# A hybrid encoder on one Trainium2 core: probabilities transposed one chunk of keys at a time for both heads, and wider dead products at the start

## The chip, the cores and the metric

One core of one Trainium2 chip runs the whole program. TensorE multiplies and transposes, and writes PSUM; VectorE, ScalarE and GpSimd do elementwise work; SyncE starts the transfers. The metric is the device time of one execution in microseconds. An engine takes its instructions in the order in which they were written; between engines, semaphores hold an instruction back until its operands are there.

## What is computed

Two layers of an encoder over a prompt of 512 tokens and a sample of 256, with 1024 features, fp32. In each layer 16 query heads of 64, two to a key head, are split among three mixers: global attention, neighbourhood attention with a learned bias, and attention over three dilated windows. Then come an output projection and a gated feed-forward part.

```python
def encoder_trunk(x, ...):
    for l in range(DEPTH):
        h = rms_norm(x, norm_mix[l])
        proj = h @ w_in[l]
        q, k, v = ...                          # 16 query heads, 8 key and value heads
        o_a = dense_block_attention(q_a, k_a, v_a)              # all keys
        o_b, _ = gathered_block_attention(q_b, k_b, v_b, na_idx, bias_b)
        branches = [gathered_block_attention(q_c, k_c, v_c, idx, bias) for (idx, bias) in dil]
        o_c = ...                              # merged by the softmax denominators
        y = jnp.concatenate([rms_norm(o, out_gain) for o in (o_a, o_b, o_c)], axis=-1)
        x = x + y @ w_out[l]
        h = rms_norm(x, norm_ffn[l])
        gate, up = jnp.split(h @ w_gate_up[l], 2, axis=-1)
        x = x + (jax.nn.silu(gate) * up) @ w_down[l]

def block(qi):                                 # 128 queries
    s = jnp.einsum('bqhgd,bkhd->bhgqk', qi, k) * scale
    p = jax.nn.softmax(s, axis=-1)
    return jnp.einsum('bhgqk,bkhd->bqhgd', p, v)
```

## The kernel before

The 768 tokens lie in three passes p of 256: p = 0 and 1 are the prompt, p = 2 is the sample. A *group* g is one key head with its two query heads h; a layer has eight, and the program takes the three neighbourhood groups first (mixer m = 1), then the three dilated ones (m = 2), then the two global ones (m = 0). Every fp32 number that enters a product is split into a high part, rounded to the type fp32r, and the rest, so a projection is three products (`mm3`, L617 to L619).

For each group `emit_qkv` makes queries, keys and values: 48 products of 256 columns for each pass, norms and rotation on VectorE, ScalarE and GpSimd, then transposes of the queries (L885) and keys (L889). `emit_attn` (L905 on) does the attention of a group, pass by pass. For a head h and a block j of 128 queries it forms the scores over 256 or 512 keys (L953, two products), finds the maximum on VectorE (L959; L997 for the masked mixers, which writes the masked scores into a tile P) and takes the exponential on ScalarE (L961 or L1000) into P. When both blocks of a head have their P, two chunks of 128 keys of both blocks are transposed into one bank of PSUM (L1012, four transposes, pool PT), ScalarE copies the bank rounded (L1019), VectorE subtracts that from the bank (L1020; both in a buffer of pool PTS), and four products of 256 columns (L1034) multiply the values with these probabilities:

```python
                        for z, c in enumerate(cs):
                            ...
                            v = vals(gs, pp)[:, jj]
                            for i in range(2):
                                end = z == len(cs) - 1 and i == 1
                                PE.matmul(po[0][:, o:o + wd], v, ps_[i][:, z * wd:(z + 1) * wd],
```

The values carry their high part and their rest side by side, so the result has 128 rows, which ScalarE (L1044) and VectorE (L1049) add up; a spread of the softmax sums (L1061) scales it. In the neighbourhood groups the two blocks of a prompt pass see different keys: two chunks are common, and each block has a third of its own, a group of one chunk and one block with products of 128 columns. The output projection of a mixer follows its last group (L617 to L619 from `yt`), with sums of squares by products with ones (L626 exact, L637 split). Then come the feed-forward products of 384 columns.

Pools matter for the order: two banks for scores (S), two for transposes (PT), one for the attention's result (PO), two for projections (D), one for small things (M); four P tiles, three PTS buffers. The order is no one's by hand: every operation is given to a planner (`Plan`) with a priority and an assumed cost, which places operations on the engines at build time, allots buffers, and writes each engine's list once. So any change of an operation moves others. The last group of a layer has no next projection beside it.

At the start, TensorE multiplies a tile of ones by itself 26 times (`warmup`, L543, `WARM`), 128 columns each, before any operand has arrived; nothing reads the result. VectorE sets the ones (L536).

Of the kernel before, what the change touches and what calls it, by code (L numbers as in the profile page):

```python
# [27 lines left out]
FIRST_F = 2  # L28
EPS = 1e-6
NEG = -1e30  # L30
WARM = 26
NSTK = 1
RW = 127
GROUPS = ((0, 1), (2, 3, 4), (5, 6, 7))
# [337 lines left out]
def trunk(ctx: ExitStack, tc: tile.TileContext, t):  # L372
# [127 lines left out]
    def ew(n, fn, r=(), w=(), prio=0.0, on="DVE POOL", act=None, fast=False, ptr=False, sbuf=True, extra=0):  # L500
        cost = {"DVE": v_cost(n, fast, ptr), "POOL": g_cost(n), "ACT": a_cost(n, sbuf, extra)}
        eng = {"DVE": DVE, "POOL": POOL}
        if on in K:
            turn[on] = turn.get(on, -1) + 1
            lst = K[on].split(",")
            on = lst[turn[on] % len(lst)]
        opts = [(e, cost[e], lambda e=e: fn(eng[e])) for e in on.split() if e != "ACT"]
        if "ACT" in on:
            opts.insert(0 if on.startswith("ACT") else len(opts), ("ACT", cost["ACT"], act))
        return P.op(opts, 0.0, None, r, w, prio, lat=0.05, lock=sbuf)  # L510

    def pe(cost, fn, r=(), w=(), prio=0.0):
        return P.op("PE", cost, fn, r, w, prio, lat=0.1)
# [22 lines left out]
    P.op("DVE", 0.2, lambda: DVE.memset(ones.bitcast(F32), 1.0), w=["ones"], prio=-100)  # L536
    act(128, lambda: ACT.copy(identr, tmp[0]), r=[tmp], w=["identr", "ident"], prio=-15)

    warm = P.buf("M")

    def warmup():
        for _ in range(WARM):
            PE.matmul(warm[0][:, 0:128], ones, ones, start=True, stop=True)  # L543

    P.op("PE", 4.0, warmup, r=["ones"], w=[warm], prio=-100)

    def load_gains(l, m, prio):
        b = P.buf("QKG")
# [254 lines left out]
    def vals(gs, p):  # L803
        return (gs[p][4 + p] if p < 2 else gs[p][3]).rearrange("p (j d) -> p j d", j=2)
# [100 lines left out]
    def emit_attn(l, g, gs, bs, mc):  # L905
# [15 lines left out]
        for p in order(g):  # L921
# [14 lines left out]
            po = P.buf("PO")  # L936
            rsum = P.buf("SM")
            rv = lambda rsum=rsum: rsum[0][:, 0:4].rearrange("p (j h) -> p j h", j=2)
            for h in range(2):
                PP = []  # L940
                for j in range(2):
                    b = 2 * p + j
                    k0, nk = 0, ncols
                    if m == 1 and p < 2:
                        k0, nk = (0, 64, 192, 256)[b], 256
                    S, pr_, mx = P.buf("S"), P.buf("P"), P.buf("SM")
                    PP.append(pr_)

                    def qk(p=p, h=h, j=j, k0=k0, nk=nk, S=S):
                        q = query(gs, p).rearrange("p (h t) -> p h t", h=2)[:, h, j * 128:(j + 1) * 128]  # L950
# [19 lines left out]
                    else:  # L970
# [29 lines left out]
                    act(nk, lambda dst=dst, mx=mx, rsl=rsl: ACT.activation(  # L1000
                        dst(), dst(), AF.Exp, bias=mx[0][:, 0:1], scale=-1.0, accum_out=rsl()),
                        r=[mx, "table"], w=[pr_, (rsum, j, h)], prio=pr, extra=2)
                grps = [((c, c + 1), (0, 1)) for c in range(0, nch - 1, 2)]
                if m == 1 and p < 2:
                    grps = [((p, p + 1), (0, 1)), ((2 - 2 * p,), (1 - p,))]
                for gi, (cs, js) in enumerate(grps):
                    n = 128 * len(cs) * len(js)
                    pt, ps_ = P.buf("PT"), P.buf("PTS")

                    def tr(cs=cs, js=js, pt=pt, PP=PP):  # L1010
                        for i, (c, j) in enumerate([(c, j) for c in cs for j in js]):
                            PE.transpose(pt[0][:, i * 128:(i + 1) * 128], PP[j][0][:, c * 128:(c + 1) * 128], ident)  # L1012

                    rr_ = [PP[j] for j in js] + [(PP[j], 1) for j in js if m == 1 and p < 2 and p != j]
                    pe(n / 128 * TR, tr, r=rr_ + ["ident"], w=[pt], prio=pr)
                    vt = [(gs[pp], "v", pp, i) for pp in ((0, 1) if p < 2 else (2,)) for i in range(2)]
                    ew(n, lambda E, n=n, pt=pt, ps_=ps_: E.tensor_copy(ps_[0][:, :n], pt[0][:, :n]), r=[pt],
                       w=[(ps_, 0)], prio=pr, sbuf=False, on="pth",
                       act=lambda n=n, pt=pt, ps_=ps_: ACT.copy(ps_[0][:, :n], pt[0][:, :n]))  # L1019
                    dve(n, lambda n=n, pt=pt, ps_=ps_: DVE.tensor_tensor(  # L1020
                        ps_[1][:, :n], pt[0][:, :n], ps_[0][:, :n].bitcast(F32), op=OP.subtract),
                        r=[pt, (ps_, 0)], w=[(ps_, 1)], prio=pr)

                    def pv(cs=cs, js=js, ps_=ps_, h=h, p=p, po=po, c0=c0, first=gi == 0, last=len(js) < 2 or gi == len(grps) - 1,
                           more=gi < len(grps) - 1 and len(grps[gi + 1][1]) < 2):
                        wd = 128 * len(js)
                        o = h * 256 + js[0] * 128
                        for z, c in enumerate(cs):
                            kb = c0 + c
                            pp, jj = (kb // 2, kb % 2) if p < 2 else (2, c)  # L1030
                            v = vals(gs, pp)[:, jj]
                            for i in range(2):
                                end = z == len(cs) - 1 and i == 1
                                PE.matmul(po[0][:, o:o + wd], v, ps_[i][:, z * wd:(z + 1) * wd],  # L1034
                                          start=first and z == 0 and i == 0, stop=end and (last or more),
                                          **({} if wd > 128 else {"skip_group_check": True}))

                    pe(2 * len(cs) * (len(js) * 128 / 2400.0 + 0.0135), pv, r=[(ps_, 0), (ps_, 1)] + vt, w=[po], prio=pr)
            yr = P.buf("Y")
            ys[m, p].append(yr)  # L1040
            for h in range(2):
# [391 lines left out]
```

## Time and profile before

| | |
|---|---|
| three runs | 1723.49, 1723.81 (median) and 1727.6 us |
| the profiled execution | 1724.8 us |
| its span, first to last instruction | 1722.9 us |
| TensorE busy | 1687.9 us (98%), 11434 products |
| VectorE, ScalarE, GpSimd busy | 1390.4, 943.7, 614.1 us |
| transfers | 145.31 MB, 84 GB/s on average |

The page gives busy times by engine, the timeline gives starts, and a wait is put down to the operation whose semaphore came last. Attention takes from about 43 to 345 us in layer 0 and from about 895 to 1203 us in layer 1; the rest is the start and the two feed-forward parts. A product's listed time overlaps with the next one's, so the distance between two starts is what one adds to TensorE's stream. Where two engines' waits meet, the one named need not be the only cause.

### The profile page before, as it was taken

What the parts mean: (1) busy time and instruction counts of PE and PEld (TensorE: products, weight loads), DVE (VectorE), ACT (ScalarE), POOL (GpSimd) and SP (SyncE); (2) the same over time, 40 slices, a digit from 0 to 9 for tenths busy, and PEclk for the clock granted to TensorE, in tenths of its full rate; (3) what the DMA queues carried; (4) which work ended last, traced back from release to release, by engine and by line L of the source; (5) the groups of instructions that cost most, each with busy time, mean ns of one, the idle gap of its engine ahead of it and who ended that gap; (6) DMA issues with size and microseconds to landing.
All of it is one profiled execution on the core that took longest, in us unless ns stands there. A gap on an engine that the chain in (4) does not pass through costs nothing. (4 is left out here: it accounts for less than half of the span.)

```text
span 1722.9 us, 31174 instructions
## 1 busy us (share of the span) xinstructions
PE 1687.9 (98%) x11434; PEld 1660.9 (96%) x11434; DVE 1390.4 (81%) x2609; ACT 943.7 (55%) x2194; POOL 614.1 (36%) x620
## 2 busy tenths in 40 slices
PE   9999999899999999999999999998999999999999
PEld 8999999899999999999999999997999999999999
DVE  7778678699988887778868886877999887868693
ACT  7877577574444444424458865866744444434230
POOL 1655254223433333224126633632242333323130
PEclk9999999999999999999999999999999999999999
DMA  6221111102433333524322201101133333334233
GB/s 182 73 69 39 38 47 40 50 31 89 132 99 103 97 103 112 155 57 130 97 64 65 77 25 38 57 26 50 47 126 101 102 101 102 108 116 138 80 111 99
DMA packets 102890, 145.31 MB, mean 84 GB/s; under 512 B 29008, under 2 KB 66896, under 8 KB 102736
## 3 DMA queue, kind: packets, MB, share of 16 engines
q1 hardware_dynamic: 102736, 143.31, 27.7%
q8 instruction: 90, 1.47, 0.4%
q14 instruction: 64, 0.52, 0.1%
HBM read 122.82 MB, written 20.45 MB: 83 GB/s over the span
## 5 line engine op out<-in xcount | busy, mean ns | idle before, releaser
L617 PE MATMUL ps<-u,w 128*128 128x384 f32 (+1 forms) x1588 | 526.8, 332 | 8.4 <-ACT y L1193 4.2
L618 PE MATMUL ps<-u,w 128*128 128x384 f32 (+1 forms) x1588 | 525.8, 331 | 0.0
L619 PE MATMUL ps<-u,w 128*128 128x384 f32 (+1 forms) x1588 | 525.6, 331 | 0.0
L617 PEld LDWEIGHTS ps<-u,w 128*128 128x128 f32 x1588 | 298.5, 188 | 11.9 <-ACT y L1193 6.4
L618 PEld LDWEIGHTS ps<-u,w 128*128 128x128 f32 x1588 | 298.5, 188 | 0.3 <-POOL u L1218 0.3
L619 PEld LDWEIGHTS ps<-u,w 128*128 128x128 f32 x1588 | 298.5, 188 | 0.0
L617 PE MATMUL ps<-w,u 128*128 128x256 f32 x768 | 227.1, 296 | 0.4 <-DVE ppa L835 0.2
L618 PE MATMUL ps<-w,u 128*128 128x256 f32 x768 | 219.4, 286 | 0.9 <-DVE w L593 0.7
L619 PE MATMUL ps<-w,u 128*128 128x256 f32 x768 | 219.2, 285 | 0.0
L618 PEld LDWEIGHTS ps<-w,u 128*128 128x128 f32 x768 | 148.6, 193 | 3.0 <-DVE w L593 2.0
L617 PEld LDWEIGHTS ps<-w,u 128*128 128x128 f32 x768 | 148.2, 193 | 2.1 <-DVE ppa L835 0.4
L592 ACT CAST w<-raw 128x1024 fp32r<-128x1024 f32 (+2 forms) x86 | 78.1, 908 | 129.6 <-PE ps L618 90.6
L619 PEld LDWEIGHTS ps<-w,u 128*128 128x128 f32 x768 | 148.4, 193 | 0.2
L1198 DVE TENSOR_TENSOR y<-y,ps 128x384 f32<-128x384 f32 x160 | 86.0, 548 | 59.9 <-PE ps L619 33.1
L617 PE MATMUL ps<-yt,w 128*128 128x256 f32 x392 | 114.1, 291 | 2.1 <-DVE x L1104 1.6
L1020 DVE TENSOR_TENSOR u<-ps,u 128x512 fp32r<-128x512 f32 (+1 forms) x160 | 98.2, 625 | 20.0 <-ACT u L1019 19.1
L618 PE MATMUL ps<-yt,w 128*128 128x256 f32 x392 | 111.8, 285 | 1.1 <-POOL yt L1090 0.8
L619 PE MATMUL ps<-yt,w 128*128 128x256 f32 x392 | 111.2, 284 | 0.0
L1034 PE MATMUL ps<-u 128*128 128x256 f32 (+1 forms) x592 | 102.9, 291 | 6.0 <-DVE u L1020 4.6
L619 PE MATMUL ps<-u,yt 128*128 128x384 f32 x292 | 97.5, 334 | 0.0
L617 PE MATMUL ps<-u,yt 128*128 128x384 f32 x292 | 97.5, 334 | 0.0
L618 PE MATMUL ps<-u,yt 128*128 128x384 f32 x292 | 97.5, 334 | 0.0
(284 smaller groups left out, 3972.3 us busy)
## 6 DMA issues: line engine op xcount, KB each, us to landing
spill<-y SPq DMA_DIRECT2D x86, 192.0 KB, 2.4
raw<-in_w_gu SPq DMA_DIRECT2D x63, 256.0 KB, 2.8
raw<-in_w_in SPq DMA_DIRECT2D x30, 512.0 KB, 3.7
p<-in_w_gu SPq DMA_DIRECT2D x44, 256.0 KB, 2.8
ppa<-in_w_gu SPq DMA_DIRECT2D x39, 256.0 KB, 2.9
raw<-in_w_out SPq DMA_DIRECT2D x16, 512.0 KB, 3.6
tbm<-in_w_gu SPq DMA_DIRECT2D x30, 256.0 KB, 2.9
raw<-in_w_down SPq DMA_DIRECT2D x16, 384.0 KB, 3.4
```

The lines of the kernel that those rows point to most:

```text
L592: act(n, lambda raw=raw, hs=hs: ACT.copy(self.flat(0)[:, hs], raw[0][:, :n]), r=[raw], w=[(b, 0) + z], prio=pr)
L617: PE.matmul(out, a[0], b[0], start=start, stop=False, skip_group_check=on)
L618: PE.matmul(out, a[0], b[1], start=False, stop=False, skip_group_check=on)
L619: PE.matmul(out, a[1], b[0], start=False, stop=stop, skip_group_check=on)
L1020: dve(n, lambda n=n, pt=pt, ps_=ps_: DVE.tensor_tensor(ps_[1][:, :n], pt[0][:, :n], ps_[0][:, :n].bitcast(F32), op=OP.subtract), r=[pt, (p ...
L1034: PE.matmul(po[0][:, o:o + wd], v, ps_[i][:, z * wd:(z + 1) * wd], start=first and z == 0 and i == 0, stop=end and (last or more), **({} i ...
L1198: dve(HALF, lambda sg=sg, dst=dst, src=src, op=op, b=bank[bn]: DVE.tensor_tensor(sg[dst], sg[src], b[0][:, :HALF], op=op), r=[bank[bn], (s ...
```

## The change

The two heads of a pass now share the transposes. Scores and exponentials are made for all four blocks (two heads, two blocks), and then one chunk of keys at a time is transposed for both heads and both blocks: four transposes into a bank as before, but with one and the same piece of the values to multiply, so two products of 512 columns take the place of four of 256. The own chunks of the neighbourhood blocks are done for both heads at once, in two products of 256 columns in place of four of 128. The lists of P tiles become `PP[h][j]`, and the loop over groups moves out of the loop over heads. The dead products take 512 columns of a tile of ones in a buffer of pool YT, set by VectorE (a new memset), and there are 15 of them.

```diff
-WARM = 26
+WARM = 15
...
-    warm = P.buf("M")
+    warm, wide = P.buf("M"), P.buf("YT")
...
         for _ in range(WARM):
-            PE.matmul(warm[0][:, 0:128], ones, ones, start=True, stop=True)
-
-    P.op("PE", 4.0, warmup, r=["ones"], w=[warm], prio=-100)
+            PE.matmul(warm[0], ones, wide[0], start=True, stop=True)
+
+    P.op("DVE", 0.35, lambda: DVE.memset(wide[0].bitcast(F32), 1.0), w=[wide], prio=-100)
+    P.op("PE", 4.0, warmup, r=["ones", wide], w=[warm], prio=-100)
...
+            PP = [[], []]
             for h in range(2):
-                PP = []
                 for j in range(2):
...
-                    PP.append(pr_)
+                    PP[h].append(pr_)
...
-                grps = [((c, c + 1), (0, 1)) for c in range(0, nch - 1, 2)]
-                if m == 1 and p < 2:
-                    grps = [((p, p + 1), (0, 1)), ((2 - 2 * p,), (1 - p,))]
-                for gi, (cs, js) in enumerate(grps):
-                    n = 128 * len(cs) * len(js)
-                    pt, ps_ = P.buf("PT"), P.buf("PTS")
-
-                    def tr(cs=cs, js=js, pt=pt, PP=PP):
-                        for i, (c, j) in enumerate([(c, j) for c in cs for j in js]):
-                            PE.transpose(pt[0][:, i * 128:(i + 1) * 128], PP[j][0][:, c * 128:(c + 1) * 128], ident)
...
+            grps = [(c, (0, 1)) for c in range(nch)]
+            if m == 1 and p < 2:
+                grps = [(p, (0, 1)), (p + 1, (0, 1)), (2 - 2 * p, (1 - p,))]
+            for gi, (c, js) in enumerate(grps):
+                full, n = len(js) == 2, 256 * len(js)
+                pt, ps_ = P.buf("PT"), P.buf("PTS")
+
+                def tr(c=c, js=js, pt=pt, PP=PP):
+                    for i, (h, j) in enumerate([(h, j) for h in range(2) for j in js]):
+                        PE.transpose(pt[0][:, i * 128:(i + 1) * 128], PP[h][j][0][:, c * 128:(c + 1) * 128], ident)
...
+                    out = po[0] if full else po[0].rearrange("p (h t) -> p h t", h=2)[:, :, js[0] * 128:js[0] * 128 + 128]
+                    for i in range(2):
+                        rhs = ps_[i][:, :n] if full else ps_[i][:, :n].rearrange("p (h t) -> p h t", h=2)
+                        PE.matmul(out, v, rhs, start=first and i == 0, stop=last and i == 1,
+                                  **({} if full else {"skip_group_check": True}))
+
+                pe(2 * (n / 2400.0 + 0.0135), pv, r=[(ps_, 0), (ps_, 1)] + vt, w=[po], prio=pr)
```

The planner's order moves with it. In these rows ps_73 and ps_74 are the banks of scores, ps_75 and ps_76 those of transposes, ps_77 the attention's result, ps_78 the small bank, ps_71 and ps_72 those of projections. In the changed kernel the scores are L954, the transposes L1013, the value products L1034, the spread L1060, and projections L618 to L620.

First place, TensorE, layer 0, last group, pass 0. Before:

```order
L953 MATMUL ps_74<-u 128x512 x2
L1061 MATMUL ps_78<-identr,sq 128x128 x2
L953 MATMUL ps_73<-u 128x512 x2
L1012 MATMUL ps_75<-identr,p 128x128 x4
L1012 MATMUL ps_76<-identr,p 128x128 x4
L953 MATMUL ps_74<-u 128x512 x2
L953 MATMUL ps_73<-u 128x512 x2
L1034 MATMUL ps_77<-u 128x256 x8
```

With the change:

```order
L1060 MATMUL ps_78<-identr,sq 128x128 x2
L954 MATMUL ps_73<-u 128x512 x2
L954 MATMUL ps_74<-u 128x512 x2
L1013 MATMUL ps_75<-identr,p 128x128 x4
L1013 MATMUL ps_76<-identr,p 128x128 x4
L954 MATMUL ps_73<-u 128x512 x2
L1034 MATMUL ps_77<-u 128x512 x2
L1013 MATMUL ps_75<-identr,p 128x128 x4
L1034 MATMUL ps_77<-u 128x512 x2
L1013 MATMUL ps_76<-identr,p 128x128 x4
L627 MATMUL ps_78<-sq,ones 128x256
L1034 MATMUL ps_77<-u 128x512 x4
```

Before, the transposes between the scores belong to the first head alone, and the last of the second head's scores stand behind them. Now all four blocks' scores of the pass stand ahead of the first transposes (the pair into ps_74 just ahead of them is already the next pass's), and value products alternate with single rows of transposes.

Second place, TensorE, layer 1, first group, between its first and second pass. Before:

```order
L1034 MATMUL ps_77<-u 128x256 x4
L1012 MATMUL ps_75<-identr,p 128x128 x4
L1034 MATMUL ps_77<-u 128x128 x2
L1012 MATMUL ps_76<-identr,p 128x128
L953 MATMUL ps_74<-u 128x256 x2
L1061 MATMUL ps_78<-identr,sq 128x128 x2
L953 MATMUL ps_73<-u 128x256 x2
L617 MATMUL ps_72<-w,u 128x256
L618 MATMUL ps_72<-w,u 128x256
L619 MATMUL ps_72<-w,u 128x256
```

With the change:

```order
L1013 MATMUL ps_76<-identr,p 128x128 x2
L1034 MATMUL ps_77<-u 128x512 x2
L954 MATMUL ps_73<-u 128x256 x2
L1034 MATMUL ps_77<-u 128x2x128 x2
L954 MATMUL ps_73<-u 128x256 x2
L1060 MATMUL ps_78<-identr,sq 128x128 x2
L954 MATMUL ps_74<-u 128x256 x2
L1013 MATMUL ps_75<-identr,p 128x128 x4
L1013 MATMUL ps_76<-identr,p 128x128 x4
L954 MATMUL ps_73<-u 128x256 x2
L1013 MATMUL ps_75<-identr,p 128x128 x2
L1034 MATMUL ps_77<-u 128x512 x4
```

Before, nine more projection products and a score pair follow the ten rows' last before the next pass's transposes. Now no projection product stands between the passes' transposes.

## Rows read from the trace of the kernel before

**Rows 1.** The page, part 1: busy time, share of the span and instructions.

```profile
PE 1687.9 (98%) x11434; PEld 1660.9 (96%) x11434; DVE 1390.4 (81%) x2609; ACT 943.7 (55%) x2194; POOL 614.1 (36%) x620
```

**Rows 2.** Stretches: length, busy time by engine (x instructions), granted clock, DMA, GB/s.

```profile
14.50:20.50 6.00, 6.00 (x30) 6.00 (x30) 6.00 (x16) 6.00 (x16) 0.00 (x0) 1.00 1.00 334
...
321.00:340.00 19.00, 15.09 (x97) 12.02 (x96) 16.64 (x28) 16.02 (x37) 6.98 (x8) 1.00 0.32 110
...
905.00:928.00 23.00, 20.97 (x176) 20.27 (x174) 19.67 (x56) 19.26 (x60) 14.43 (x23) 1.00 0.33 80
```

**Rows 3.** Groups by shape: tiles, shape, count; busy, mean ns; idle before, releasers.

```profile
L1034 PE MATMUL ps<-u 128*128 128x256 f32 x544 | 93.4, 292 | 6.0 <-DVE u L1020 4.6 <-DVE y L1049 1.2
...
L1000 ACT ACTIVATE p<-p,sm 128x256 f32<-128x256 f32 x96 | 48.6, 508 | 8.4 <-DVE sm L997 8.0
...
L1034 PE MATMUL ps<-u 128*128 128x128 f32 x48 | 9.7, 283 | 0.0
```

**Rows 4.** TensorE's timeline: start us, us, engine, line, what; layer 0, layer 1.

```profile
308.42 0.64 PE L1034 MATMUL ps<-u 128*128 128x256 f32 x4
308.90 0.28 PE L617 MATMUL ps<-yt,w 128*128 128x256 f32 x1
...
321.35 0.63 PE L953 MATMUL ps<-u 128*128 128x512 f32 x2
321.81 0.38 PE L1061 MATMUL ps<-identr,sq 128*128 128x128 f32 x2
...
336.71 0.28 PE L618 MATMUL ps<-yt,w 128*128 128x256 f32 x1
...
905.52 0.60 PE L1012 MATMUL ps<-identr,p 128*128 128x128 f32 x4
905.88 0.42 PE L1034 MATMUL ps<-u 128*128 128x128 f32 x2
906.13 0.30 PE L1012 MATMUL ps<-identr,p 128*128 128x128 f32 x1
```

**Rows 5.** TensorE's timeline, the start of the program.

```profile
1.09 5.81 PE L543 MATMUL ps<-ones 128*128 128x128 f32 x26 [1.09 <-DVE ones L536]
...
20.03 0.41 PE L618 MATMUL ps<-w,u 128*128 128x256 f32 x1
20.25 0.41 PE L619 MATMUL ps<-w,u 128*128 128x256 f32 x1
...
21.16 0.28 PE L619 MATMUL ps<-w,u 128*128 128x256 f32 x1
21.28 0.28 PE L617 MATMUL ps<-w,u 128*128 128x256 f32 x1
...
33.66 0.54 PE L885 MATMUL ps<-identr,u 128*128 128x128 f32 x4 [1.34 <-DVE u L877]
```

**Rows 6.** VectorE's timeline, the start of the program.

```profile
23.08 0.29 DVE L839 TENSOR_TENSOR vs<-ps,rbt 128x128 f32<-128x128 f32 x1 [1.99 <-ACT ppa L834]
```

**Rows 7.** Timelines of TensorE and VectorE, last group of layer 0.

```profile
326.40 0.73 PE L953 MATMUL ps<-u 128*128 128x512 f32 x2 [1.18 <-ACT p L961]
...
328.73 1.04 PE L1012 MATMUL ps<-identr,p 128*128 128x128 f32 x8
...
337.78 0.60 PE L1012 MATMUL ps<-identr,p 128*128 128x128 f32 x4
...
339.04 0.69 DVE L1020 TENSOR_TENSOR u<-ps,u 128x512 fp32r<-128x512 f32 x1 [1.28 <-ACT u L1019]
```

**Rows 8.** Waits of TensorE: total us, times, longest; 310:340, 905:928, 1174:1200.

```profile
PE ps L1012 <- ACT p L961: 1.9, 2, 1.0
PE ps L1034 <- DVE u L1020: 1.2, 2, 0.8
...
PE ps L953 <- DVE sm L997: 1.7, 1, 1.7
...
PE ps L1034 <- DVE u L1020: 1.7, 2, 1.5
```

More of the change, by code (lines that the diff above doesn't have):

```diff
@@ L1002, in emit_attn @@
                         r=[mx, "table"], w=[pr_, (rsum, j, h)], prio=pr, extra=2)
-                grps = [((c, c + 1), (0, 1)) for c in range(0, nch - 1, 2)]
-                if m == 1 and p < 2:
-                    grps = [((p, p + 1), (0, 1)), ((2 - 2 * p,), (1 - p,))]
-                for gi, (cs, js) in enumerate(grps):
-                    n = 128 * len(cs) * len(js)
-                    pt, ps_ = P.buf("PT"), P.buf("PTS")
-                    def tr(cs=cs, js=js, pt=pt, PP=PP):
-                        for i, (c, j) in enumerate([(c, j) for c in cs for j in js]):
-                            PE.transpose(pt[0][:, i * 128:(i + 1) * 128], PP[j][0][:, c * 128:(c + 1) * 128], ident)
[L1014 to L1038, printed above, removed]
@@ new lines, in emit_attn, with pv @@
+            grps = [(c, (0, 1)) for c in range(nch)]
[7 more added lines that the diff above has]
+                        PE.transpose(pt[0][:, i * 128:(i + 1) * 128], PP[h][j][0][:, c * 128:(c + 1) * 128], ident)
+                rr_ = [PP[h][j] for h in range(2) for j in js]
+                rr_ += [(PP[h][j], 1) for h in range(2) for j in js if m == 1 and p < 2 and p != j]
+                pe(n / 128 * TR, tr, r=rr_ + ["ident"], w=[pt], prio=pr)
+                vt = [(gs[pp], "v", pp, i) for pp in ((0, 1) if p < 2 else (2,)) for i in range(2)]
+                ew(n, lambda E, n=n, pt=pt, ps_=ps_: E.tensor_copy(ps_[0][:, :n], pt[0][:, :n]), r=[pt],
+                   w=[(ps_, 0)], prio=pr, sbuf=False, on="pth",
+                   act=lambda n=n, pt=pt, ps_=ps_: ACT.copy(ps_[0][:, :n], pt[0][:, :n]))
+                dve(n, lambda n=n, pt=pt, ps_=ps_: DVE.tensor_tensor(
+                    ps_[1][:, :n], pt[0][:, :n], ps_[0][:, :n].bitcast(F32), op=OP.subtract),
+                    r=[pt, (ps_, 0)], w=[(ps_, 1)], prio=pr)
+                last = gi == len(grps) - 1 or len(grps[gi + 1][1]) < 2
+                def pv(c=c, js=js, ps_=ps_, p=p, po=po, c0=c0, first=gi == 0, last=last, full=full, n=n):
+                    kb = c0 + c
+                    pp, jj = (kb // 2, kb % 2) if p < 2 else (2, c)
+                    v = vals(gs, pp)[:, jj]
+                    out = po[0] if full else po[0].rearrange("p (h t) -> p h t", h=2)[:, :, js[0] * 128:js[0] * 128 + 128]
[4 more added lines that the diff above has]
+                pe(2 * (n / 2400.0 + 0.0135), pv, r=[(ps_, 0), (ps_, 1)] + vt, w=[po], prio=pr)
```

## The prediction

> **What bounds the kernel now.** I read the page first: TensorE is busy for 98% of the span [rows 1], so what a change is worth depends on what it does to the stream of products, and on the few places where that stream waits. The page's busy time counts the pipeline of a product too (a product of 256 columns is listed with 0.28 us, yet the next one starts 0.12 us later [rows 5]), so I went on to the starts in the timeline, which show what a product costs on the path. Then I looked for waits, stage by stage. In the feed-forward stretches TensorE hardly waits. The attention stretches do wait, most of all in the last head group of a layer, where no projection of a next group is left to fill the gaps [rows 7, 8], and in the first group of layer 1 [rows 8]. There VectorE is busy for 19.67 and ScalarE for 19.26 of 23 us [rows 2], so what TensorE waits for comes through two engines that have little room. The third place is the start.
>
> **Value products.** There are 544 of 256 columns, in 136 groups of four, and 48 of 128 columns, in 24 pairs [rows 3]. Four of 256 take 0.48 us from start to the next start; the scores' two of 512 columns take 0.46 us, and they are what each group becomes [rows 4]. By these rows the change saves 0.02 us x 136 = 2.7 us. The stamps have two digits, so I also take the step apart: 0.12 us, less 256 columns at the 2.4 GHz level (0.107 us), leaves 0.013 us per product, and 272 products go: 3.6 us. I take 3.2. The Trainium skill (TensorE: Matmul & The Clock Gate, "Back-to-back issue gap") gives a fixed part of about 2.5 ns beside the columns instead; by that the term would be 272 x 0.0025 = 0.7 us and the time 2.5 us later than I forecast. The trace does not agree: its step leaves 13 ns, not 2.5.
>
> The 24 pairs of 128 columns become 12 pairs of 256, since one product now takes the odd block for both heads. A pair of 128 takes 0.25 us [rows 4], no less than a pair of 256 does (0.24), so narrow products save nothing by being narrow: 24 x 0.25 - 12 x 0.24 = 3.1 us. Some pairs stand closer in the trace; were they all at the columns alone (2 x 0.053 us), the term would be -0.3 us. I take 3.0. All of this lies on the path, because TensorE is the bound around it. Transposes keep their number. Copies and differences out of PSUM become 12 fewer pieces on ScalarE and VectorE each; I cost that at nothing, as both have other work beside it.
>
> **Dead products at the start.** Before, 26 dead products of 128 columns end near 6.9 us; real products then step by 0.21 to 0.22 us until about 20.5 us and by 0.12 us afterwards [rows 2, 5]. The granted-clock column prints 1.00 there [rows 2], so it does not tell these apart; 256 columns in 0.21 us is the 1.2 GHz level, in 0.12 us the 2.4 GHz level. The dead products too ran at the lower level (0.22 us for 128 columns), and the step fell only after some 6 us of products of 256 columns back to back. Fifteen of 512 columns at the lower level, 0.43 us each, fill 6.4 us without a break in the columns, so I expect the level to rise by their end. They start a little later (a VectorE memset of 512 columns comes ahead; VectorE is idle then, waiting for the gains' transfer) and end 1 us later at worst, which the operands' lateness until 14 us absorbs.
>
> What is that worth? From 14.5 to 20.5 us VectorE and ScalarE are busy without a gap [rows 2], and TensorE is the late one: 30 products step by 0.21 instead of 0.12 us, 2.8 us. Behind it VectorE stands idle for 1.99 us, waiting for ScalarE's square of the first group [rows 6], which cannot begin before that group's last product. After that VectorE has hardly a gap until the transposes of the first queries, which start at 33.66 us after a wait of 1.34 us for it [rows 5]. So only VectorE's 1.99 us can be gained there; the rest turns into a longer wait at those transposes. I take 2.0 us, with ends of 0 (no rise) and 3.0.
>
> **What is added: later transposes.** The first transpose of a pass now needs the exponentials of both heads, four blocks instead of two. All four P tiles come free only with the pass's last transposes, so the next pass's exponentials start later. Where other products stand between, that costs nothing; the cover is the projection of the next group, and where that is gone TensorE waits. The needs, from rows: from the end of a pair of 512-column scores to its transpose 2.33 - 0.46 = 1.87 us; from the end of four transposes to their difference on VectorE 1.95 us from the first transpose's start [rows 7], less the 0.36 us that four take [rows 4], 1.6 us. From one pass's last transposes to the next's first in the neighbourhood groups: landing and first reduction some 0.8 us, then four exponentials of 0.51 us [rows 3], about 2.9 us, an estimate.
>
> *Last group, layer 0* (first place of the order). Behind the 512-column scores stands one further pair (0.46 us) ahead of the transposes: 1.4 us short. The first value products have four transposes and a score pair ahead of them, 0.82 us: 0.8 short; the third, counted alike, 0.94 us: 0.7 short; the fourth another 0.3. The second pass lacks some 1.2. Together 4.4 us, against 3.1 us of waits of the transposes and value products shown before [rows 8]. In layer 1 the same count gives about 3 us, against 1.7 us shown there for the differences alone [rows 8]. Waits come out longer than such counts when the two engines serve other work first, so I put 1.0 us for both tails, with ends of -2 and +4.
>
> *First group of layer 1* (second place). Between the last transposes of one pass and the first of the next stand a pair of 512 (0.46 us), four pairs of 256 (0.24 each) and a spread (some 0.1), 1.5 us in all, where 2.9 are needed: 1.4 short. Then the first value products have 0.78 us of the needed 1.6: 0.8 short. One wait of 1.7 us shown there now may go. I put 1.5 us, ends 0 and 3.
>
> *Elsewhere.* Seven more passages between passes of the neighbourhood groups have a cover that exceeds the need by less than 0.6 us. ScalarE and VectorE also serve the next group's projections, so an exponential there may be late: 0.3 us each, 2.0 us, ends 0 and 6.
>
> **The sum.** -3.2 - 3.0 - 2.0 + 1.0 + 1.5 + 2.0 = -3.7 us. The profiled execution took 1724.8 us (span 1722.9), so 1721.1 us; the median of the three runs, 1723.81, is 1.0 us below that execution. A measurement tells about 0.3%, 5.2 us, from no change.
>
> **Rivals.** *Cover holds:* the scheduler puts the transposes where nothing waits, as it does in most groups before, and no net wait is added: 1724.8 - 8.2 = 1716.6. For it: only two passages lack cover by the count. Against it: tails already wait now. Chance 0.26.
>
> *The P tiles become the bound (slower):* a pass's four exponentials, four copies and four differences must then run through within one pass, since the next has no P tile to write. It decides where TensorE's work between passes is shorter than the chain in its real, queued length; with a chain 1.5 us longer than my 2.9, the seven narrow passages wait some 1.2 us each and the two that lack cover 2.9 and 1.7, 13 us, and the tails cost the 1.0 of above: 1724.8 - 8.2 + 14 = 1730.6. For it: VectorE and ScalarE are 84% busy there. Against it: most passages have over 4 us of cover. Chance 0.14.
>
> *The dead products do not do what they are for:* the level stays low until 20 us, or falls again at 8 to 14 us, where products wait for operands. Then 2.0 us are missing: 1723.1. Against a fall: in the tail of layer 0 TensorE is busy for only 15.09 of 19 us [rows 2], and a product of 256 columns is still listed with 0.28 us [rows 4], not with the 0.41 us of the lower level [rows 5]. Chance 0.15.
>
> **Chances.** My forecast has the remaining 0.45. Faster by over 0.3% means under 1718.6: the first rival and the lower part of the forecast's spread, 0.36. Slower means over 1729.0: the second rival and a little of the rest, 0.16. Within: 0.48. For the range, the low end takes the first rival with its starting term at 3.0 and 1 us of luck, 1714.5; the high end stops short of the slower rival's centre, 1729.5, which leaves out about 0.1 on each side.
>
> **What would show it.** Value products in pairs with 0.45 to 0.46 us from start to start of two; no pair of 128 columns; a step of 0.12 us by 9 us; the first query transposes near 31.5 us; waits of the transposes on exponentials (p) in the first group of layer 1, about 2 us. I am wrong if pairs of 512 take 0.48 or more, if the step is still 0.21 us at 15 us, or if waits on p turn up in all neighbourhood groups.

## The result and the profile after

The changed kernel takes 1742.41 us (median of 4 runs, 1741.67 to 1743.19); the kernel before took 1724.61 beside it. The ratio is 1.0102, 95% interval 1.009 to 1.0115: slower, and outside the predicted range. The profiled execution took 1743.19 us, span 1741.2, so 18.3 us more of span than before.

The page of the changed kernel, part 1:

```profile
PE 1695.2 (97%) x11127; PEld 1650.6 (95%) x11127; DVE 1405.9 (81%) x2612; ACT 941.8 (54%) x2184; POOL 595.1 (34%) x604
```

307 products are gone [rows 1], and yet TensorE's busy time grew by 7 us, so some products ran longer. The stretches show where (columns as in [rows 2]):

```profile
14.50:20.50 6.00, 6.00 (x32) 6.00 (x31) 6.00 (x16) 5.90 (x16) 0.00 (x0) 0.54 0.98 327
321.00:340.00 19.00, 16.02 (x97) 12.41 (x96) 17.02 (x32) 17.01 (x42) 8.99 (x10) 1.00 0.37 111
905.00:928.00 23.00, 20.48 (x146) 18.26 (x145) 17.56 (x50) 16.96 (x50) 8.90 (x17) 0.93 0.19 45
345.00:900.00 555.00, 544.33 (x3270) 541.93 (x3269) 460.14 (x741) 242.32 (x474) 160.72 (x125) 0.98 0.32 97
```

The same 555 us of the feed-forward in the kernel before:

```profile
345.00:900.00 555.00, 549.00 (x3360) 545.77 (x3359) 463.70 (x759) 251.04 (x494) 168.10 (x133) 1.00 0.33 98
```

Ninety records of TensorE fewer fit into the same stretch, which the diff doesn't touch, and the granted clock there is 0.98. What the prediction looked for is there too. The value products by shape, and one set in the timeline (two of 512 columns, 310.75 to 311.22):

```profile
L1034 PE MATMUL ps<-u 128*128 128x512 f32 x272 | 90.7, 414 | 1.8 <-DVE u L1022 1.5 <-DVE y L1048 0.2
...
L1034 PE MATMUL ps<-u 128*128 128x256 f32 x24 | 5.4, 300 | 0.8 <-DVE u L1022 0.6 <-ACT u L1021 0.2
```

```profile
310.75 0.63 PE L1034 MATMUL ps<-u 128*128 128x512 f32 x2
311.22 0.62 PE L954 MATMUL ps<-u 128*128 128x512 f32 x2
```

The start, in TensorE's timeline:

```profile
1.62 5.92 PE L543 MATMUL ps<-yt,ones 128*128 128x512 f32 x15 [1.62 <-DVE yt L545]
7.39 0.27 PE L618 MATMUL ps<-w,u 128*128 128x256 f32 x1
7.50 0.28 PE L619 MATMUL ps<-w,u 128*128 128x256 f32 x1
...
14.58 0.41 PE L619 MATMUL ps<-w,u 128*128 128x256 f32 x1
14.79 0.41 PE L620 MATMUL ps<-w,u 128*128 128x256 f32 x1
...
33.07 0.53 PE L886 MATMUL ps<-identr,u 128*128 128x128 f32 x4 [1.83 <-DVE u L878]
```

The wide dead products do raise the level: at 7.5 us a product of 256 columns steps by 0.12 us. Then operands are late, and from 14 to 20 us the step is 0.21 again, the 1.2 GHz level. The first query transposes start 0.6 us earlier than before [rows 5], not 2.

The largest single loss stands in the first feed-forward. TensorE's, VectorE's and GpSimd's timelines of the changed kernel:

```profile
800.33 0.34 PE L620 MATMUL ps<-u,yt 128*128 128x384 f32 x1
805.64 0.66 PE L618 MATMUL ps<-u,w 128*128 128x384 f32 x1 [4.98 <-DVE x L1258]
806.10 0.53 PE L619 MATMUL ps<-u,w 128*128 128x384 f32 x1
806.42 0.53 PE L620 MATMUL ps<-u,w 128*128 128x384 f32 x1
```

```profile
797.54 0.68 DVE L1134 TENSOR_TENSOR w<-p,w 128x512 fp32r<-128x512 f32 x1
...
799.07 1.69 DVE L1134 TENSOR_TENSOR w<-raw,w 128x512 fp32r<-128x512 f32 x1
800.68 1.75 DVE L1134 TENSOR_TENSOR w<-p,w 128x512 fp32r<-128x512 f32 x1
802.35 1.74 DVE L1134 TENSOR_TENSOR w<-raw,w 128x512 fp32r<-128x512 f32 x1
804.02 1.01 DVE L1236 TENSOR_TENSOR u<-tbm,u 128x384 fp32r<-128x384 f32 x2
804.96 0.54 DVE L1258 TENSOR_TENSOR x<-x,ps 128x384 f32<-128x384 f32 x1
```

```profile
798.92 1.29 POOL L1134 TENSOR_TENSOR w<-p,w 128x512 fp32r<-128x512 f32 x1 [4.13 <-ACT w L1133]
800.48 1.40 POOL L1134 TENSOR_TENSOR w<-raw,w 128x512 fp32r<-128x512 f32 x1 [0.28 <-ACT w L1133]
801.84 1.71 POOL L1134 TENSOR_TENSOR w<-ppa,w 128x512 fp32r<-128x512 f32 x1
```

TensorE has filled a bank and waits for VectorE to add it to x (L1258). From 799.07 us VectorE has three splits of weights (L1134) and two subtractions (L1236, 1.01 us together) ahead of that addition, and each split takes 1.7 us instead of 0.68: GpSimd runs the same operation beside it, and VectorE's ends 0.54 to 0.55 us after GpSimd's each time (800.76 after 800.21, 802.43 after 801.88, 804.09 after 803.55). After the wait 384 columns step by 0.32 us instead of 0.17. Another such wait of 4.06 us ends at 1672.15 us. In the kernel before, the longest waits of this kind are 1.62 and 1.59 us:

```profile
818.19 0.41 PE L617 MATMUL ps<-u,w 128*128 128x384 f32 x1 [1.62 <-DVE x L1259]
```

**Lost time by stage.** To compare orders I summed, over TensorE's timeline, each distance between two starts less the step of its kind at the upper level (0.120 us for 256 columns, 0.173 for 384, 0.227 for 512, at most 0.089 for the 128-column ones). What is left is waits, small gaps and slow steps. (0.227 is low: a value product of 512 columns behind which nothing waits steps by 0.233 us, the median of 57 pairs ahead of transposes. What that changes is said where it matters.) One profiled execution each, in us:

| kernel | 0–40 | 40–345 attention | 345–900 | 900–1260 attention | 1260– | sum |
|---|---|---|---|---|---|---|
| before | 13.6 | 23.4 | 11.6 | 27.0 | 6.8 | 82.4 |
| changed | 13.1 | 22.5 | 22.3 | 33.9 | 12.6 | 104.4 |

The products' own steps add up to 1635.2 us before and 1630.9 now; with 0.2335 us for 512 columns they are 2.4 us apart instead of 4.3. So 16.5 of the 22 us lost stand outside attention.

### The profile page after: what moved, and what is told of

Same layout as the page of the kernel before. It is cut to its first block, busy times and chain, and to the rows that moved or that the text cites. A ratio compares the mean times of both kernels' runs of the same rounds, so it can differ in the third digit from the quotient of the medians.

```text
span 1741.2 us, 30428 instructions
## 1 busy us (share of the span) xinstructions
PE 1695.2 (97%) x11127; PEld 1650.6 (95%) x11127; DVE 1405.9 (81%) x2612; ACT 941.8 (54%) x2184; POOL 595.1 (34%) x604
## 5 line engine op out<-in xcount | busy, mean ns | idle before, releaser
L618 PE MATMUL ps<-u,w 128*128 128x384 f32 (+1 forms) x1584 | 528.0, 333 | 14.0 <-DVE x L1258 10.0
L620 PE MATMUL ps<-u,w 128*128 128x384 f32 (+1 forms) x1584 | 526.1, 332 | 0.0
L618 PEld LDWEIGHTS ps<-u,w 128*128 128x128 f32 x1584 | 299.4, 189 | 17.4 <-issue 11.1
L620 PEld LDWEIGHTS ps<-u,w 128*128 128x128 f32 x1584 | 299.1, 189 | 0.0
L618 PE MATMUL ps<-w,u 128*128 128x256 f32 x768 | 229.3, 299 | 3.6 <-DVE x L1302 1.6
L620 PE MATMUL ps<-w,u 128*128 128x256 f32 x768 | 219.9, 286 | 0.0
L618 PEld LDWEIGHTS ps<-w,u 128*128 128x128 f32 x768 | 148.9, 194 | 6.5 <-DVE x L1302 1.8
L620 PEld LDWEIGHTS ps<-w,u 128*128 128x128 f32 x768 | 148.9, 194 | 0.3 <-DVE u L654 0.2
L618 PE MATMUL ps<-yt,w 128*128 128x256 f32 x392 | 114.4, 292 | 0.9 <-ACT yt L1088 0.8
L620 PE MATMUL ps<-yt,w 128*128 128x256 f32 x392 | 111.8, 285 | 0.0
L954 PE MATMUL ps<-u 128*128 128x256 f32 (+1 forms) x384 | 93.9, 344 | 6.1 <-ACT p L962 3.0
L618 PE MATMUL ps<-u,yt 128*128 128x384 f32 x296 | 99.3, 335 | 0.0
L619 PE MATMUL ps<-u,yt 128*128 128x384 f32 x296 | 99.3, 335 | 0.0
L620 PE MATMUL ps<-u,yt 128*128 128x384 f32 x296 | 99.3, 335 | 0.0
```

The lines of the kernel that those rows point to most:

```text
L618: PE.matmul(out, a[0], b[0], start=start, stop=False, skip_group_check=on)
L619: PE.matmul(out, a[0], b[1], start=False, stop=False, skip_group_check=on)
L620: PE.matmul(out, a[1], b[0], start=False, stop=stop, skip_group_check=on)
L954: PE.matmul(S[0][:, :nk], q, kk[:, k0:k0 + nk], start=i == 0, stop=i == 1)
```

## The experiments

Two theories. *Order*: the planner plans the whole program up to 16 times (`PASSES`) with priorities taken from the last attempt, and keeps the one that its own estimate likes best: its fourth before, its ninth now. The edit makes it write another order everywhere, and that order is bad in the feed-forward. *Work*: the joined products or the dead products cost the time themselves. Ratios are to the kernel before, beside which each ran (1724.6 to 1725.6 us). Brackets hold the ratio and its 95% interval.

**One part alone.** The assumed costs of the dead products don't change, so the first kernel has the changed kernel's order, the second that of before.

```diff
-WARM = 15
+WARM = 26
...
-            PE.matmul(warm[0], ones, wide[0], start=True, stop=True)
+            PE.matmul(warm[0][:, 0:128], ones, ones, start=True, stop=True)
```

> The value products and transposes of the change, with the old dead products (26 of 128 columns). The planner assumes the same cost for both kinds of dead products, so every engine's order is that of the changed kernel. If the order and its waits cost the time (and the lower TensorE level that follows waits): 1738 to 1744 us, with the level low again after the waits near 400, 805, 873, 925, 1211 and 1672 us. If the wide dead products put the clock into a state in which it falls more easily: no such stretches, and 1724 to 1730 us.

> The kernel before with the new dead products alone (15 of 512 columns); the order is that of the kernel before. If the order costs the time: 1721 to 1725 us, with no low stretch after 45 us; at the start the level rises by 7 us and falls again near 13 us, so nothing is gained there. If the wide dead products are the cause of the falls: low stretches after the waits near 322, 816, 867 and 1201 us, and 1730 to 1740 us.

Measured: the attention part alone 1737.32 us (1.007, 1.0055 to 1.0085), the dead products alone 1725.2 (0.9999, 0.9989 to 1.0008). The loss comes with the attention part or its order. The first lies a little under the 1738 us of theory order, and its level is low after the waits near 800, 916, 1206 and 1667 us, but not near 400 and 873; the second lies 0.2 us over its range, with one low stretch at 328 us that was not expected. The dead products gain 1.5 us before 40 us (12.1 lost instead of 13.6) and give that back in the attention of layer 0 (24.9 instead of 23.4). In the changed order they even cost 5.1 us. Where some of that goes, one place shows in both kernels, which have one order. First the changed kernel, then the attention part alone:

```profile
872.52 0.39 PE L618 MATMUL ps<-w,u 128*128 128x256 f32 x1 [1.61 <-DVE x L1302]
...
873.98 1.01 PE L691 MATMUL ps<-ones,yt 128*128 128x2 f32 x4 [0.49 <-DVE ept L699]
874.86 0.56 PE L618 MATMUL ps<-w,u 128*128 128x256 f32 x1
875.22 0.41 PE L619 MATMUL ps<-w,u 128*128 128x256 f32 x1
875.43 0.41 PE L620 MATMUL ps<-w,u 128*128 128x256 f32 x1
```

```profile
868.65 0.39 PE L617 MATMUL ps<-w,u 128*128 128x256 f32 x1 [1.61 <-DVE x L1301]
...
870.11 0.60 PE L690 MATMUL ps<-ones,yt 128*128 128x2 f32 x4 [0.49 <-DVE ept L698]
870.58 0.36 PE L617 MATMUL ps<-w,u 128*128 128x256 f32 x1
870.78 0.28 PE L618 MATMUL ps<-w,u 128*128 128x256 f32 x1
870.90 0.28 PE L619 MATMUL ps<-w,u 128*128 128x256 f32 x1
```

The same two waits, 1.61 and 0.49 us; in the one the level falls, and until 880 us the products step by 0.21 us; in the other it holds, at 0.12. By the granted-clock column, read microsecond by microsecond, the changed kernel spends 38 us at the lower level, 31 of them after 20 us; the attention part alone 20.5 and the kernel before none after its start, where the column of these two prints 1.00. By the steps a microsecond there does 0.12/0.21 of the work, so 31 against 20.5 us makes some 4.7 of the 5.1 us, an estimate.

**Orders of the feed-forward exchanged.** All operations of the second norms and the feed-forward are taken from the other kernel's order; each engine's list is written from a table of numbers, with the attention as in its own kernel.

```diff
+        raw = zlib.decompress(base64.b85decode(TABLE))
+        v = struct.unpack("<%dI" % (len(raw) // 4), raw)
+        for a, s in zip(v[::2], v[1::2]):
+            o = self.ops[a // 5]
```

> The changed kernel's work; the order in attention and projections is its own, but the second norm and the feed-forward part stand in the order of the kernel before (a table replaces the planner). If the waits of the feed-forward order are the main cost: 1724 to 1730 us, without the low stretches near 400, 805 and 1672 us. If the time is lost to late transposes in attention and only shows up later: 1738 to 1743 us.

> The reverse: the kernel before, its attention and projections in their own order, with the second norm and the feed-forward part in the order of the changed kernel. If the feed-forward order is the main cost: 1735 to 1742 us, with low stretches near 400, 805, 870 and 1670 us. If attention is: 1722 to 1727 us.

Measured: 1761.72 us (1.0211, 1.0194 to 1.0228) and 1763.65 (1.0229, 1.0211 to 1.0246). Both lie outside both ranges. The totals decide nothing, since both lose at the seams where two orders meet (one wait of 18.0 us at the end of the first feed-forward). Inside, the waits follow the order, not the work: from 800 to 840 us TensorE loses 2.5 us with the change and before's order, and 8.4 with before's work and the changed order.

So the table was mended: the planner runs, and holds only the norms' and feed-forward's operations to their engines, slots and mutual order; the seams are its own.

```diff
+                    if o.seq in self.fixed:
+                        if e != self.fixed[o.seq][0] or self.lists[e][at[e]] != o.seq:
+                            continue
```

> The whole change, with the operations of the second norms and the feed-forwards held to the engines, slots and relative order that they have in the kernel before, and everything else (attention, projections, the seams between them) placed by the planner around them. Theory order (the loss comes from the new order that the planner writes for the feed-forward): the interior waits of PE go back to those of before (at 800 to 840 us and at 1640 to 1700 us about 3 us each instead of 8), with clean seams, and the time is 1718 to 1730 us. Rival work (the joined products themselves cost, by what they leave behind for the stretches after them): 1737 to 1746 us.

Measured: 1728.59 us, 1.0016 (1.0006 to 1.0026). Of the 17.8 us of the change, some 14 are gone, as theory order has it. Its attention stands in another order too, so the stages matter: it loses 11 us less than the changed kernel from 345 to 900 us, 3.6 less from 1260 us on and 2.0 less before 40 us, and 0.9 more in attention. Its waits of TensorE from 780 to 900 us, where the changed kernel has one of 5.0 us, begin with those of before:

```profile
PE ps L653 <- DVE x L1293: 2.1, 2, 1.6
```

**Other orders of the same work.** The kernels are untouched but for the attempt that the planner keeps.

```diff
-            if best is None or span < best[0]:
+            if i == KEEP:
```

> The work of the kernel before, unchanged; only the order is another one, that of the planner's fifth attempt instead of its fourth. Theory order: another order of the same work can cost as much as the change did, with waits of several us on the accumulation of the feed-forward and a lower clock after them: 1730 to 1745 us. Rival work: the work is that of before, so the time is within 4 us of it, 1722 to 1730 us.

> The work of the changed kernel, unchanged; the order is that of the planner's fourth attempt instead of its ninth. Theory order: the time differs from the change's 1742 by more than 5 us, and where the long waits stand (the accumulation of the feed-forward at 800 and 1668 us) is different. Rival work: 1738 to 1746 us, with the same loss in the same stretches.

> The work of the changed kernel, unchanged; the order is that of the planner's fourteenth attempt. Theory order: as for the fourth attempt, a time that differs from 1742 by more than 5 us, and from the fourth attempt's as well. Rival work: 1738 to 1746 us.

> The work of the changed kernel, unchanged, in the order of the planner's fifth attempt. Theory order: one more draw of the same lot as the ninth, fourth and fourteenth (1742, 1730, 1733): 1722 to 1740 us, with the loss where waits stand in its own order. Rival work: 1738 to 1746 us.

> The work of the kernel before in the order of the planner's third attempt. Theory luck (the edit itself is worth its 5 to 7 us, and its orders so far were only worse draws than the two of before): before's other orders spread as widely as the change's, 1720 to 1742 us, with a middle above 1727. Rival grouping (taking a chunk for both heads at once costs PE more waits in any order than the products save): before's orders stay at 1718 to 1727 us, under all five of the change (1729 to 1742).

> The work of the kernel before in the order of the planner's sixth attempt. As for the third: luck 1720 to 1742 us, grouping 1718 to 1727 us.

> The work of the changed kernel in the order of the planner's third attempt. Luck: at least one of this and the sixth attempt is at 1725 us or less. Grouping: both are at 1728 us or more.

> The work of the changed kernel in the order of the planner's sixth attempt. As for the third: luck one of the two at 1725 us or less, grouping both at 1728 us or more.

| attempt | work of before: us, ratio (interval) | work of the change |
|---|---|---|
| 3rd | 1740.39, 1.0088 (1.0073–1.0103) | 1737.77, 1.0077 (1.0062–1.0092) |
| 4th | the kernel before, 1725 | 1730.21, 1.0031 (1.0018–1.0045) |
| 5th | 1719.65, 0.9965 (0.9951–0.9979) | 1730.51, 1.0031 (1.002–1.0042) |
| 6th | 1726.85, 1.0011 (1.0001–1.0021) | 1738.28, 1.0075 (1.0059–1.0091) |
| 9th | | the change, 1742.41 |
| 14th | | 1733.5, 1.0049 (1.0034–1.0064) |

The order alone moves equal work by 20.7 us (before) and 12.2 us (the change): as much as the change did. I had expected the fifth attempt for before to be slower; it lies under both ranges and is faster than both kernels, with as many products on TensorE as before [rows 1]. The fourteenth for the change is only 3.3 us from the fourth, not the 5 expected. Of the last four, before's third (1740.39) is what luck forecast and grouping excluded; the change's third and sixth, both over 1728, are what grouping forecast and luck excluded. Neither theory stands alone. TensorE and the other engines in the fifth attempt for before:

```profile
PE 1687.5 (98%) x11434; PEld 1662.8 (97%) x11434; DVE 1389.2 (81%) x2610; ACT 941.2 (55%) x2193; POOL 606.0 (35%) x620
```

The third attempt for before shows the changed kernel's loss without the change. Its longest waits, from 780 to 900 us and from 1600 us on:

```profile
PE ps L618 <- ACT w L593: 5.2, 1, 5.2
```

```profile
PE ps L618 <- ACT w L593: 3.5, 1, 3.5
```

They stand near the same two places, late in each feed-forward, with another cause: ScalarE rounds weights whose transfer came late. ScalarE's timeline there:

```profile
833.68 1.04 ACT L593 CAST w<-raw 128x1024 fp32r<-128x1024 f32 x1 [5.26 <-DMA raw<-in_w_down]
```

**The joined products by themselves.** In the version with the feed-forward held, the products are cut again by head; every engine's list stays as it was. The running sums of the two heads then start in turn within one bank and don't come out whole; all products are issued.

```diff
-                    for i in range(2):
-                        rhs = ps_[i][:, :n] if full else ps_[i][:, :n].rearrange("p (h t) -> p h t", h=2)
-                        PE.matmul(out, v, rhs, start=first and i == 0, stop=last and i == 1,
-                                  **({} if full else {"skip_group_check": True}))
+                    wd = 128 * len(js)
+                    for h in range(2):
+                        o = h * 256 + js[0] * 128
+                        for i in range(2):
+                            PE.matmul(po[0][:, o:o + wd], v, ps_[i][:, h * wd:(h + 1) * wd], start=first and i == 0, stop=last and i == 1,
+                                      skip_group_check=True)
```

> The version with the feed-forward held in the order of before (1728.6 us), and the order of every engine exactly as there; only the value products are cut again by head: four of 256 columns instead of two of 512, and four of 128 columns instead of two of 2x128 on the odd neighbour chunks. Theory products (the terms of the prediction for the products, 3.2 and 3.0 us, are paid on the path that sets the end): slower than that version by 4 to 7 us, 1732 to 1736 us. Rival cover (the products stand where PE waits for something else anyway): within 2 us of 1728.6.

Measured: 1735.76 us (1.006, 1.0047 to 1.0072) against 1728.59: 7.2 us, in the range of theory products and clear of rival cover. How much of it is the products themselves, the rows tell one by one, since the two traces have one order: where nothing waits, 126 sets of four of 256 columns take 0.0138 us longer each than two of 512, and 12 sets of four of 128 columns 0.16 us longer than two of 2x128, 3.7 us together. (By the fixed steps above it would be 4.6 us, 1636.5 against 1631.9.) The rest stands in waits and slow stretches, among them a fall of the level at 872 us that the joined version doesn't have. By the Trainium skill (TensorE: Matmul & The Clock Gate, "Back-to-back issue gap"), with its 2.5 ns a product, an estimated 0.7 us would have come. The rows do not agree.

**Combinations.** The change with the feed-forward held as above, by the numbers of before's fifth attempt in place of the fourth's; and that fifth attempt (`KEEP = 4`, counted from 0) with the wide dead products:

```diff
-WARM = 26
+WARM = 15
...
-            PE.matmul(warm[0][:, 0:128], ones, ones, start=True, stop=True)
+            PE.matmul(warm[0], ones, wide[0], start=True, stop=True)
```

> The whole change, with the operations of the second norms and the feed-forwards held to the order that they have in the fifth attempt of the planner for the kernel before (1719.7 us) instead of the fourth. Theory order: the stretches of the feed-forward wait as little as there (about 3 us from 360 to 880 and 1 us from 1640 on beside 2 at 800), and the time is 1719 to 1727 us; with the saved products, 5 us, under 1719.7 only if attention waits no more than there. Rival work: as the version with before's fourth order or slower, 1728 to 1735 us.

> The kernel before in the order of the planner's fifth attempt (1719.7 us), with the 15 dead products of 512 columns alone: the order is the same on every engine. Theory start (the wide dead products raise the clock level before the first projections, worth 1 to 2.5 us at the start as in the versions with 11 to 12 us of waits there): 1717 to 1719 us. Rival (the level falls back at 13 us, nothing is gained): 1718.5 to 1721 us.

Measured: 1734.58 us (1.0052, 1.0037 to 1.0068) and 1721.74 (0.9981, 0.9972 to 0.999). Theory order missed the first, and rival work, 1728 to 1735 us, has it; the second lies above both of its ranges. In the first the feed-forward is indeed good at the end (4.3 us lost from 1260 us on), but the attention of layer 1 loses 37.1 us ahead of it. In the second the start gains 1.7 us (11.5 lost instead of 13.2) and the total is 2.1 us above the same order without them, though the intervals overlap.

**What grouping costs.** Mean lost time of the four orders of before's work, and of the eight of the change's work with its own dead products and whole products (the two with the feed-forward held among them):

| | 0–40 | 40–345 | 345–900 | 900–1260 | 1260– | sum | steps | time |
|---|---|---|---|---|---|---|---|---|
| before's work, 4 orders | 13.2 | 22.9 | 14.1 | 28.2 | 7.2 | 85.6 | 1634.9 | 1728.0 |
| the change's, 8 orders | 11.8 | 25.7 | 15.9 | 32.5 | 8.8 | 94.7 | 1631.6 | 1734.5 |

Attention loses 7.1 us more with the heads joined by this count. Some 1.8 us of that is no loss but the step of 272 products of 512 columns, 0.2335 us and not 0.227; then the two sets overlap from 900 to 1260 us (the least of the eight 28.8, the most of before's four 29.3). The other 5.3 us aren't mostly waiting: the waits that the timeline names in attention grow by 1.7 us on average. The lower level is the other part: from 40 to 345 and 900 to 1260 us it holds for 11.5 us on average, against 3.4, and at 0.12/0.21 of the work that is some 3.5 us, an estimate. The eight also have the wide dead products, and before's four do not; by themselves these moved the attention of layer 0 from 23.4 to 24.9 us above, so not all of the difference need come from grouping. In the tail of layer 0, with the feed-forward held:

```profile
325.94 1.91 PE L1048 MATMUL ps<-identr,p 128*128 128x128 f32 x8
327.50 1.20 PE L989 MATMUL ps<-u 128*128 128x512 f32 x2
328.50 0.99 PE L1069 MATMUL ps<-u 128*128 128x512 f32 x2
```

Eight transposes take 1.56 us there, where four took 0.36 [rows 4]. The means of the times differ by 6.5 us, with a spread of 20.7 us among the four and 13.8 among the eight, so the sign of the edit itself is likely, not settled. That grouping makes TensorE pause in larger pieces, and so lets the level fall, fits these rows; no run isolated it.

## Why the prediction was wrong

- **The step that failed is the one that isn't in the sum.** "In the feed-forward stretches TensorE hardly waits" was true of the kernel before, and the sum carried it over, though any change of an operation moves others in the planner's lists, and the prediction read the new lists in attention alone. The profiled pair loses 16.5 us more outside attention (345 to 900 and from 1260 us): in the new order VectorE's additions that free a bank come late, with waits of 4.98 and 4.06 us where 1.62 was the longest, and slow steps follow. In these stretches the waits that the timeline names grow by 8.2 us, and the granted clock is low for 21 us, before never. Holding the old order there takes 14 us back, and before's work has the same loss in another order. No rival had this mechanism, so the range couldn't hold it.
- **Value products, -3.2 and -3.0.** The first has the right sign and is too large, the second is right. Where nothing waits, four of 256 columns took 0.482 us before and two of 512 take 0.469 now (medians of 125 sets each), 136 x 0.013 = 1.8 us: a product of 512 columns steps by 0.233 us, 20 ns beside its columns, not the 13 taken from the 256-column ones. Pairs of 128 columns took 0.254 us and the pairs of 2x128 take 0.242 (medians): 24 x 0.254 - 12 x 0.242 = 3.2 us.
- **Dead products, -2.0.** Mis-sized: nothing. The level rose, as said, and fell again while products waited, which the third rival had; at 15 us the step is 0.21 us, the prediction's own sign of being wrong. The 1.5 us that the dead products alone gain at the start are given back later. The argument against a fall, that it held in the tail of layer 0 before, was too weak: that very tail falls in other orders.
- **Tails, +1.0.** The first tail (320 to 345 us) lost 6.4 us instead of 7.4, the second (1160 to 1260) 10.5 instead of 10.0: about -0.5, within its ends (the count of short covers gave +2.6, and 1.0 was put). The waits on exponentials that had been counted came, smaller. TensorE's waits from 310 to 345 us:

```profile
PE ps L954 <- ACT p L962: 1.1, 1, 1.1
PE ps L1013 <- ACT p L962: 0.8, 1, 0.8
```

- **First group of layer 1 and elsewhere, +1.5 and +2.0.** Layer 0 shows nothing (16.0 and 16.1 us lost from 40 to 320), layer 1 +6.4 us from 900 to 1160 (17.0, now 23.4; some 0.9 of it is the step of 512 columns), more than the 3.5 put and less than the 9 of the upper ends together. In the first group transposes do wait for p, for less than the 1.4 us counted (L1001 below), beside a fall of the level at 924 us. TensorE's waits from 900 to 930 us:

```profile
PE ps L954 <- DVE sm L998: 0.9, 1, 0.9
PE ps L1034 <- DVE u L1022: 0.6, 1, 0.6
PE ps L1013 <- ACT p L1001: 0.6, 1, 0.6
```

- **The P tiles as the bound, 1730.6.** Near the time of several orders of the change, but not by that mechanism: waits on p did not turn up in all groups (in layer 0 from 40 to 320 us they make 0.4 us). The 84% given there for both engines is ScalarE's; VectorE's 19.67 of 23 us are 86%.

By steps, with 0.2335 us for 512 columns, for the profiled pair: products -2.4 (the dead ones, which take longer than before, among them), start -0.5, attention +4.1, outside attention +16.5; together 17.7 of the 18.3 us of span.

## What to carry to other kernels

Where a planner writes the whole order, an edit is a new draw of it everywhere. Count the edit's own terms, but look for the range in how much equal work spreads over the planner's orders (here 12 to 21 us, several times the edit's worth), and read the stretches that the diff doesn't touch in the order too, above all what stands ahead of each addition that frees a bank of TensorE. Before crediting or blaming such an edit, time two or three orders of either work: here that alone gave 1719.65 us, faster than both kernels, without any change of the work.

## What the runs showed of the hardware

- The level of TensorE's clock can fall in the middle of a kernel: here behind waits of 1.61 and 0.49 us, and then the steps are long until 880 us. Equal waits in an equal order let it fall in one kernel and not in the other, which differs in its dead products alone (steps of 0.21 or 0.12 us, above). Executions of one kernel differ along with the granted clock: the change's sixth attempt took 1734.44 us at 0.994 and 1740.21 at 0.991.
- The granted-clock column prints 1.00 at the start of the kernel before [rows 2], where steps show the lower level, and 0.54 in the same stretch of the changed kernel, where it had risen and fallen: read the steps.
- A VectorE subtraction of two 512-column operands in SBUF takes 0.68 us alone and 1.69 to 1.75 beside GpSimd's, and it ends 0.55 us after GpSimd's instruction does (median of 71 such subtractions in the changed kernel that began while GpSimd was running), as if it waited that one out. The Trainium skill (GPSIMD Engine Reference, "Specifications") says that the two share their SBUF interfaces, with contention when VectorE has two inputs there. The trace agrees: in the changed kernel 157 VectorE operations on 384 columns with an operand in PSUM, such as the additions to x, began at least 0.2 us before a GpSimd instruction ended, and all took 0.53 to 0.56 us, as they do alone.
